# Fifteen pairs of projection tiles by seven block products instead of eight

## The chip, the cores and the metric

The kernel runs as one launch on one core of a Trainium2 chip. The metric is device time of one execution in microseconds (us). The inputs are in DRAM as fp32 and everything is computed to fp32 accuracy: an operand of a matrix product is split in a high and a low part that TensorE multiplies at its fast fp32 rate (type fp32r), and a product is the sum of high*high, high*low and low*high.

## What is computed

One layer of a hybrid encoder on 1024 prompt tokens and 64 tokens of a running stream, 1088 columns in all. One input projection feeds two branches:

```python
qa, ka, va, za, qkv_b, a_b, b_b, z_b, g_a, g_b = in_projection(x, w_in)   # x: 1088 x 1024
oa  = window_attention(rope(qa), rope(ka), va, sinks)      # 16 q heads, 4 kv heads of 64, chunks of 64 + 2 before
y_a = (oa * silu(za)) @ w_o_attn
qb, kb, vb = split(silu(causal_conv(qkv_b)))               # branch B: gated delta rule, 8 heads of 128
y_b = (rmsnorm(delta_rule(qb, kb, vb, decay(a_b), sigmoid(b_b))) * silu(z_b)) @ w_o_delta
h   = sigmoid(g_a) * y_a + sigmoid(g_b) * y_b
y   = layer_norm(ALPHA * x + h @ w_out)
```

The query `qa`, the branch-A gate `za` and the merge gates `g_a`, `g_b` are 1024 channels wide each: 8 + 8 + 16 tiles of 128 channels.

## The kernel before

The transposed input lies in SBUF for the whole run as eight tiles `ring` of [128, 2, 1088], one for each 128 input channels (a k-tile), high part and low part. Columns go in three groups, `GROUPS` = 384, 384 and 320. A **projection tile** gives 128 output channels for all columns: `weights` loads 128x1024 weights into `wraw`, splits them into `whi` (ScalarE copy, L85) and `wlo` (VectorE subtraction, L86), and `project`/`mm3` issue 3 groups x 8 k-tiles x 3 products = 72 matmuls. All matmuls go through `mm` (L103), transposes through L106, and TensorE takes them in the order of the program. PSUM has three buffers `pj` for projections and five `bg` for the rest. The other engines' order comes from priorities (`urgent` moves work ahead).

The stages, by the time in the profile:

- **Load and keys**, to 31.7 us. x arrives and is split, two key tiles are projected, and VectorE turns them by the rope table `cs` (`rope`), 1.1 MB that is read last of the load.
- **V and a/b** (`vab`), 31.7 to 58: 208 matmuls of 272 columns whose weights were split into a buffer of the pool `pla`, the pool of x's raw data.
- **Query**, 58 to 153: 8 tiles. Each column group is copied out of PSUM, turned (a shuffle and three VectorE operations), and split into high and low parts that go to DRAM (`q_d`). `gates`, the decays of branch B, run beside the first tile.
- **Branch-A gate**, 153 to 249: 8 tiles, silu into the SBUF tile `sz`. Beside it the keys are split, stored to `k_d` and read back into an SBUF tile `kp`.
- **Attention**, 249 to 503: 36 units (two heads of two kv heads, two chunks). `attention` issues the values of unit i-2, the flip (transposes of the probabilities P) of unit i-1, the scores of unit i, and then lets `weave` fill TensorE with `UNIT` = 8797 columns of 13 merge-gate tiles while P is made: VectorE takes maxima (`mx`, `nm`), ScalarE the exponentials (L479), VectorE the sums (`smm`) and the scaling (L485). A merge gate is copied to DRAM (`gA_d`, `gB_d`).
- **Branch B**, 503 to 1209: per pair of heads, the projections and the recurrence, filled with other projections. `GATES` = (0, 1, 1, 1) puts one of the last three merge-gate tiles behind each of pairs 1, 2 and 3.
- **Output**, 1209 to 1435.

## Time and profile before

| | before |
|---|---|
| time of three runs, us | median 1438.28 (1437.5 to 1438.64) |
| profiled execution, span from first to last instruction, us | 1434.8 |
| TensorE busy, us (share of span) | 1419.5 (99%) |
| VectorE busy | 896.1 (62%) |
| ScalarE busy | 536.0 (37%) |
| GpSimd busy | 152.2 (11%) |
| bytes moved by DMA | 147.47 MB |

The span is the profiled execution's own time as the profile gives it; the median of the timed runs is 3.5 us (0.2%) above it. In the views, PE is TensorE's matmuls, PEld its weight loads, DVE VectorE, ACT ScalarE, POOL GpSimd, SP the engine that issues most transfers. "L103" is a line of the kernel. PEclk is the clock that TensorE was granted, as a share of full speed.

### The profile page before, as it was taken

How to read it: one execution, taken by the hardware profiler on the slowest of the kernel's cores; microseconds unless marked ns; L12 is line 12 of the kernel's file. 1: busy time of each engine (PE TensorE's matmuls, PEld its weight loads, DVE VectorE, ACT ScalarE, POOL GpSimd, SP SyncE). 2: the span in 40 equal slices, each digit the busy share in tenths (PEclk: the TensorE clock that was granted, in tenths of full speed). 3: DMA queues.
4: the chain of work that ended last, by engine and by line, in shares of the span. 5: the costliest groups of instructions: out<-in, count | busy, mean ns of one | idle time of the engine just before them, and what ended most of it. 6: DMA issues, size and time to landing. Idle time of an engine off the chain costs nothing.

```text
span 1434.8 us, 28644 instructions
## 1 busy us (share of the span) xinstructions
PE 1419.5 (99%) x11362; PEld 1305.7 (91%) x11362; DVE 896.1 (62%) x2216; ACT 536.0 (37%) x1480; POOL 152.2 (11%) x321
## 2 busy tenths in 40 slices
PE   8999999999999999999999999999999999999997
PEld 8999999888888899988999889988999889999886
DVE  6477522555555447966696667866697444554676
ACT  5333311444444334345543555245534332322100
POOL 0000000000000014121231214021231100000000
PEclk9999999999999999999999999999999999999999
DMA  8134571333432321110222103211436326475221
GB/s 275 39 107 169 197 185 45 101 93 95 135 97 87 122 62 40 60 47 16 78 74 74 31 24 87 91 57 32 125 105 201 99 71 190 162 220 164 93 88 74
DMA packets 81172, 147.47 MB, mean 103 GB/s; under 512 B 10896, under 2 KB 60304, under 8 KB 79760
## 3 DMA queue, kind: packets, MB, share of 16 engines
q1 hardware_dynamic: 67552, 135.17, 29.6%
q10 hardware_dynamic: 13488, 10.49, 2.4%
q8 instruction: 89, 1.46, 0.4%
q14 instruction: 43, 0.35, 0.1%
HBM read 101.39 MB, written 44.24 MB: 102 GB/s over the span
## 4 chain that ended last, share of the span: by engine, by line
PE 98%; DVE 1%; ACT 1%; issue 0%; POOL 0%; DMA 0%; DVEq 0%; SPq 0%; ACTq 0%
PE pj L103 71%; PE bg L103 22%; PE bg L106 4%; PE pj L106 1%; DMA pl<-xT 0%; ACT whi L85 0%; DVE acc L582 0%; DVE whi L978 0%; ACT P L479 0%; POOL w1k L612 0%; ACT L319 0%; POOL ncv L575 0%; DVE whi L995 0%; DVE mx L468 0%; DVEq L1176 0%
## 5 line engine op out<-in xcount | busy, mean ns | idle before, releaser
L103 PE MATMUL pj<-ring,whi 128*128 128x384 f32 (+1 forms) x3696 | 929.8, 331 | 0.0
L103 PEld LDWEIGHTS pj<-ring,whi 128*128 128x128 f32 x3696 | 649.1, 188 | 3.1 <-issue 1.8
L103 PE MATMUL pj<-ring,wlo 128*128 128x384 f32 (+1 forms) x1848 | 610.6, 330 | 0.0
L103 PEld LDWEIGHTS pj<-ring,wlo 128*128 128x128 f32 x1848 | 347.7, 188 | 1.0 <-issue 0.7
L582 DVE SCALAR_TENSOR_TENSOR acc<-pre,sm,acc 128x384 f32<-128x384 f32 (+1 forms) x216 | 137.1, 640 | 24.9 <-ACT acc L580 21.5
L86 DVE TENSOR_TENSOR wlo<-wraw,whi 128x1024 fp32r<-128x1024 f32 (+2 forms) x86 | 101.0, 1175 | 80.4 <-ACT whi L85 74.2
L85 ACT ACTIVATE whi<-wraw 128x1024 fp32r<-128x1024 f32 (+2 forms) x86 | 87.6, 1018 | 114.5 <-PE pj L103 78.9
L103 PE MATMUL pj<-pl,ring 128*128 128x512 f32 (+2 forms) x432 | 94.5, 337 | 0.0
L103 PEld LDWEIGHTS pj<-pl,ring 128*128 128x128 f32 x432 | 68.4, 188 | 8.1
L479 ACT ACTIVATE P<-bg,nm 128x192 f32<-128x192 f32 (+2 forms) x136 | 54.4, 409 | 57.1 <-DVE nm L472 57.1
L785 DVE SCALAR_TENSOR_TENSOR S<-S,dec,bg 128x128 f32<-128x128 f32 x128 | 38.7, 344 | 54.5 <-PE bg L103 53.8
L103 PE MATMUL bg<-ring,whi 128*128 128x384 f32 (+1 forms) x240 | 61.3, 338 | 4.3 <-ACT ring L85 4.3
L583 ACT ACTIVATE gt<-acc 128x384 f32<-128x384 f32 (+1 forms) x72 | 36.5, 507 | 68.6 <-DVE acc L582 67.8
L588 DVE SCALAR_TENSOR_TENSOR plb<-gt,acc 128x384 f32<-128x384 f32 (+1 forms) x96 | 44.8, 483 | 22.8 <-ACT gt L583 22.7
L564 POOL MEMSET pre<- 128x3 f32 x24 | 2.4, 100 | 524.5 <-DMA prodA<-pl 476.6
L103 PEld LDWEIGHTS bg<-ring,whi 128*128 128x128 f32 x240 | 43.8, 192 | 6.2 <-ACT ring L85 4.8
L103 PE MATMUL bg<-PT,V 128*64 128x128 f32 (+1 forms) x496 | 48.1, 296 | 0.0
L580 ACT ACTIVATE acc<-pre,sm 128x384 f32<-128x384 f32 (+1 forms) x72 | 42.9, 597 | 12.9 <-DVE r17i L94 5.0
L103 PEld LDWEIGHTS bg<-PT,V 128*64 128x64 f32 (+1 forms) x496 | 24.3, 133 | 23.4 <-issue 21.2
L103 PE MATMUL pj<-wolo,ring 128*128 128x512 f32 (+1 forms) x120 | 45.0, 375 | 0.0
L795 ACT ACTIVATE w1k<-plb 128x128 f32<-128x128 f32 x68 | 21.0, 308 | 61.3 <-DVE plb L793 50.2
L480 DVE TENSOR_TENSOR smm<-smm,es 128x4 f32<-128x4 f32 (+1 forms) x36 | 5.8, 162 | 58.8 <-ACT P L479 58.8
(225 smaller groups left out, 1839.1 us busy)
## 6 DMA issues: line engine op xcount, KB each, us to landing
wraw<-w_tiles SPq DMA_DIRECT2D x80, 512.0 KB, 3.7
q_d<-pl SPq DMA_DIRECT2D x4, 2176.0 KB, 7.7
q<-q_d SPq DMA_DIRECT2D x64, 128.0 KB, 2.9
pl<-k_d SPq DMA_DIRECT2D x8, 512.0 KB, 8.0
prodA<-pl SPq DMA_DIRECT2D x2, 2048.0 KB, 7.9
t2k<-zs_d ACTq DMA_DIRECT2D x16, 256.0 KB, 2.8
prodB<-t2k ACTq DMA_DIRECT2D x16, 256.0 KB, 3.1
wraw<-w_out SPq DMA_DIRECT2D x8, 512.0 KB, 4.1
```

What stands on the lines that cost most here:

```text
L85: self.nc.scalar.activation(hi, raw, AF.Copy)
L86: self.nc.vector.tensor_tensor(lo, raw, hi.bitcast(F32), ALU.subtract)
L103: self.tc.keep_in_program_order(self.nc.tensor.matmul(o, l, r, start=start, stop=stop))
L106: self.tc.keep_in_program_order(self.nc.tensor.transpose(o, x, self.ident))
L479: nc.scalar.activation(P[:, hf, k], ps[:, k], AF.Exp, bias=nm[:, hf, b : b + 1], scale=0.125, accum_out=sm[:, hf, b : b + 1])
L480: nc.vector.tensor_tensor(sm[:, :, :nb], sm[:, :, :nb], es[:, :, :nb], ALU.add)
L580: nc.scalar.activation(acc[:, :w], pre[:, 0:w], AF.Copy, scale=cw(0))
L582: nc.vector.scalar_tensor_tensor(acc[:, :w], pre[:, j : j + w], cw(j), acc[:, :w], ALU.mult, ALU.add)
L583: nc.scalar.activation(th[:, :w], acc[:, :w], AF.Tanh, scale=0.5)
L588: nc.vector.scalar_tensor_tensor(o, v(th), 1.0, v(acc), ALU.add, ALU.mult)
L785: nc.vector.scalar_tensor_tensor(Sn[:, h], S[:, h], self.egl[h][:, p, c : c + 1], kv[:, 0:128], ALU.mult, ALU.add)
L795: nc.scalar.activation(junk, o, AF.Square, accum_out=d["sso"][:, c : c + 1])
```

## The change

Two neighbouring tiles (256 channels) are one product of a 2x2 block matrix of weights (blocks of 128 channels x 512 inputs, a11 to a22) with a 2x2 block matrix of x (512 inputs x 272 columns, B11 to B22, for each half g of the columns). It is now made by seven block products in place of eight. Eight sums of blocks feed it: T1 to T4 from x (made once, on GpSimd, `sums_x`) and s1 to s4 from each pair's weights (on GpSimd, `weights7`). One product is 12 matmuls of 272 columns (`product`), so a pair is 2 halves x 7 products x 12 = 168 matmuls of 272 columns; before it was 144 of 384 or 320. A PSUM buffer is read in the middle of a chain of products (`keep`, ScalarE), and the copies u are added to another product when it is done (`land`, VectorE). The 8 query, 8 branch-A gate and 14 merge-gate tiles go this way, 15 pairs; the rest stays.

T1 to T3 get a pool of their own (`rp2`). T4 is written over the odd quarters of the columns of four `ring` tiles at the end of `vab`, and `restore_x` reads x again after attention. To make room, the pool `pla` is closed after the keys and `vab`'s weights and the sums' operands come in a pool `vb` that begins where `pla` was; the pools `ws` (sums and splits of weights) and `rq` (query) begin where `vb` was, and the rope table is read a second time. Keys are split and stored as they are made (`put`, 44 stores of 64 partitions), through two buffers each of `khi` and `klo`; attention reads keys, query and branch-A gate from DRAM for each unit or pair of units. `GATES` becomes (0, 1, 1, 0): the last pair's merge-gate tile moves ahead into attention.

```diff
-GATES = (0, 1, 1, 1)
+GATES = (0, 1, 1, 0)
+    def sums_x(self):
...
+        for k in range(4):
+            xr = self.t(self.vb, [128, 2, NT], "xr", bufs=2)
+            nc.sync.dma_start(xr, self.I["xT"].rearrange("(h k) p n -> k p h n", h=2)[k])
...
+            for i, x, y in ((1, b12, b11), (2, b22, tm[1]), (3, b22, b12), (4, b21, tm[2])):
+                nc.gpsimd.tensor_tensor(tm[i], x, y, ALU.subtract)
+            for i in (2, 1, 3):
+                d = self.T[i, k] = self.t(self.rp2, [128, 2, 2, HN], "ring2", F32R, bufs=12)
+                self.split(d[:, 0], d[:, 1], tm[i])
+    def weights7(self):
...
+            sub(s1, a21, a22, ALU.add)
+            sub(s2, s1, a11, ALU.subtract)
+            sub(s3, a11, a21, ALU.subtract)
+            sub(s4, a12, s2, ALU.subtract)
+            for i, x in enumerate((a11, a12, s2, s1, s3, a22, s4)):
+                pool, tag, bufs = ((self.wp, "whi", 2), (self.wp, "wlo", 2), (self.ws, "wx", 3))[(0, 1, 2, 0, 1, 2, 2)[i]]
+                w = self.t(pool, [128, KT, 128], tag, F32R, bufs=bufs)
+                self.split(w[:, :4], w[:, 4:], x)
+    def product(self, ps, w, name, g, first, last):
+        hi, lo = w
+        for k in range(4):
+            xh, xl = self.operand(name, k, g)
+            for i, (l, r) in enumerate(((hi, xh), (hi, xl), (lo, xh))):
+                self.mm(ps[:, :HN], l[:, k], r, first and k == 0 and i == 0, last and k == 3 and i == 2, True)
+                yield HN
+    def stream(self, jobs):
...
+        for evac in jobs:
+            W = self.weights7()
+            for g in range(2):
+                cols = (2 * g * HN, (2 * g + 1) * HN)
+                A = self.pjt()
+                yield from self.product(A, W[0], "B11", g, True, False)
+                p1 = keep(A)
+                if tail:
+                    yield from tail
+                B = self.pjt()
+                yield from self.product(B, W[1], "B21", g, True, True)
+                evac(0, cols[0], B[:, :HN], p1)
+                yield from self.product(A, W[2], "T2", g, False, False)
+                u2 = keep(A)
+                C = self.pjt()
+                yield from self.product(C, W[3], "T1", g, True, False)
+                yield from self.product(A, W[4], "T3", g, False, False)
+                u3 = keep(A)
+                evac(1, cols[1], C[:, :HN], u3)
+
+                def rest(evac=evac, W=W, g=g, cols=cols, A=A, C=C, u2=u2):
+                    yield from self.product(A, W[5], "T4", g, False, True)
+                    evac(1, cols[0], A[:, :HN], None)
+                    yield from self.product(C, W[6], "B22", g, False, True)
+                    evac(0, cols[1], C[:, :HN], u2)
...
     def vab(self):
-        wt = self.t(self.pl, [128, 2, KT, 272], "pl", F32R)
+        wt = self.t(self.vb, [128, 2, KT, 272], "wt", F32R)
...
+        def put(gp, src, dst):
+            n = src.shape[-1]
+            for s, part in enumerate(self.key_parts(src)):
+                for hf in range(2):
+                    nc.sync.dma_start(self.k_d[gp, :, 2 * s + hf, dst : dst + n], part[HS[hf]].bitcast(F32))
...
+    def key_parts(self, src):
+        n = src.shape[-1]
+        parts = [self.t(self.pl, [128, 384], x, F32R, bufs=2)[:, :n] for x in ("khi", "klo")]
+        self.split(*parts, src)
+        return parts
...
         for hf in range(2):
-            ps = self.pjt() if hf else self.ps()
+            ps = self.ps()
```

**First place where instructions moved: ScalarE between the keys and `vab`.** `khi`/`klo` are the key parts on their way to DRAM, `wt` (before: `pl_45`) the split of `vab`'s weights, `V` the copy of its first result. A DMAHW name is the completion count of one of the eight lanes of SP's transfers. Before:

```order
L85 ACTIVATE ring_9_97<-pl_1_89 128x320
L85 ACTIVATE pl_45_413<-wraw_46_414 128x1088 [waits DMAHW6_49]
L273 DMA gt_48_422<-cg 128x256
L273 DMA gt_49_424<-cg 128x256 [waits Activation_49]
L85 ACTIVATE pl_45_413<-wraw_47_418 128x1088 [waits DMAHW7_49]
```

Now:

```order
L87 ACTIVATE khi_51_407<-rraw_47_392 128x64 [waits DMAHW5_49,DMAHW4_49]
L87 ACTIVATE khi_56_449<-rraw_54_442 128x256 [waits DMAHW0_49,DMAHW1_49,DVE_49,Activation_49]
L87 ACTIVATE khi_58_457<-rraw_54_442 128x64 [waits DMAHW5_49,DMAHW4_49,DVE_49]
L87 ACTIVATE khi_61_469<-ck_60_467 128x128 [waits DMAHW3_49,DMAHW2_49,DVE_49]
L87 ACTIVATE khi_63_477<-ck_60_467 128x128 [waits DMAHW7_49,DMAHW6_49,DVE_49]
L87 ACTIVATE wt_65_493<-wraw_66_494 128x1088 [waits DMAHW4_49,DMAHW3_49,DMAHW5_49,DMAHW2_49,DMAHW6_49,DMAHW1_49,DMAHW7_49,DMAHW0_49,DVE_49]
L87 ACTIVATE wt_65_493<-wraw_67_498 128x1088
L417 ACTIVATE V_68_502<-pj_103_590 128x256 [waits PE_49]
```

The split of `vab`'s weights stood behind the load of x and waited for its own data; it now stands behind the last key parts and waits for all eight lanes, on which the key stores are.

**Second place: ScalarE at the first pair of query tiles.** `sums` are s1 to s4, `whi`, `wlo`, `wx` the high parts of the pair's weights, `u` the copies of partial sums. Now (nothing of this stood there before):

```order
L417 ACTIVATE V_68_502<-pj_111_806 64x256
L418 ACTIVATE abt_69_503<-pj_111_806 64x16
L431 DMA cg0_113_844<-cg 128x128
L87 ACTIVATE whi_123_870<-sums_119_856 128x512
L87 ACTIVATE wlo_124_873<-sums_119_856 128x512
L87 ACTIVATE wx_122_867<-sums_119_856 128x512
L87 ACTIVATE wx_125_876<-wraw_118_854 128x512
L87 ACTIVATE wx_126_879<-sums_119_856 128x512
L349 ACTIVATE u_128_895<-pj_127_882 128x272
```

Three splits of sums stand between the end of `vab` and the first copy `u_128`, and the one that the next product takes (`wx_122`, s2) stands third.

**Third place: ScalarE within one unit of attention.** The L479 (now L644) rows are the four exponentials of one unit, `es` a small one of the sink, `PT` the copy of the flip. Before:

```order
L438 ACTIVATE gt_336_2781<-pj_324_2706 128x384
L479 ACTIVATE P_335_2769,smm_331_2750<-bg_332_2751,nm_329_2748 128x192
L474 ACTIVATE es_330_2749<-es_330_2749 128x4
L479 ACTIVATE P_335_2769,smm_331_2750<-bg_332_2751,nm_329_2748 128x192
L479 ACTIVATE P_335_2769,smm_331_2750<-bg_333_2752,nm_329_2748 128x192 x2
L85 ACTIVATE whi_386_3065<-wraw_385_3064 128x1024
L438 ACTIVATE gt_338_2809<-pj_337_2784 128x320
```

Now, in another unit:

```order
L644 ACTIVATE P_646_4198,smm_642_4179<-bg_643_4180,nm_640_4177 128x192
L639 ACTIVATE es_641_4178<-es_641_4178 128x4
L644 ACTIVATE P_646_4198,smm_642_4179<-bg_643_4180,nm_640_4177 128x192
L349 ACTIVATE u_647_4220<-pj_596_3943 128x272
L87 ACTIVATE wlo_657_4248<-sums_652_4231 128x512
L644 ACTIVATE P_646_4198,smm_642_4179<-bg_644_4181,nm_640_4177 128x192
L349 ACTIVATE u_661_4270<-pj_660_4257 128x272
L644 ACTIVATE P_646_4198,smm_642_4179<-bg_644_4181,nm_640_4177 128x192
L571 ACTIVATE gs_649_4224<-gs_648_4222 128x272
L668 COPY PT_662_4292<-bg_663_4293 128x3x128
```

The fill's splits and copies stood behind the four exponentials; now two copies and a split stand between them.

## Rows read from the trace of the kernel before

**Rows 1.** Page, parts 1, 4 and 5: busy time, chain by engine, weight loads.
```profile
PE 1419.5 (99%) x11362; PEld 1305.7 (91%) x11362; DVE 896.1 (62%) x2216; ACT 536.0 (37%) x1480; POOL 152.2 (11%) x321
...
PE 98%; DVE 1%; ACT 1%; issue 0%; POOL 0%; DMA 0%; DVEq 0%; SPq 0%; ACTq 0%
...
L103 PEld LDWEIGHTS pj<-ring,whi 128*128 128x128 f32 x3696 | 649.1, 188 | 3.1 <-issue 1.8
```

**Rows 2.** Busy time by stage; columns: stretch, length, engines with instruction counts, clock, DMA.
```profile
31.70:58.00 26.30, 26.30 (x211) 26.30 (x210) 11.09 (x29) 6.25 (x21) 0.00 (x0) 1.00 0.12 37
58.00:153.00 95.00, 94.89 (x578) 94.57 (x577) 70.15 (x156) 33.04 (x63) 0.00 (x0) 1.00 0.32 116
153.00:249.00 96.00, 96.00 (x586) 96.00 (x585) 27.68 (x42) 22.22 (x36) 0.00 (x0) 1.00 0.54 154
249.00:503.00 254.00, 253.15 (x1882) 222.30 (x1880) 139.25 (x451) 107.16 (x403) 0.00 (x0) 1.00 0.33 104
```

**Rows 3.** Chain of waits, from 1200 to 1240: start, length, what.
```profile
1209.07 14.92 PE pj L103 x93
1223.99 12.00 PE bg L103 x72
```

**Rows 4.** Timeline of VectorE behind the keys: start, length, operation, idle before.
```profile
30.96 0.56 DVE L351 TENSOR_TENSOR rsh<-rsh,cs 128x384 f32<-128x384 f32 x1 [5.40 <-DMA cs<-rope]
31.44 0.55 DVE L352 TENSOR_TENSOR rraw<-rraw,cs 128x384 f32<-128x384 f32 x1
...
32.72 1.23 DVE L86 TENSOR_TENSOR wlo<-wraw,whi 128x1024 fp32r<-128x1024 f32 x1 [0.27 <-ACT whi L85]
...
42.52 0.56 DVE L376 TENSOR_TENSOR kT<-rraw,rsh 128x256 f32<-128x256 f32 x2
```

**Rows 5.** Transfers from 20 to 60: issues, KB each, median us to landing.
```profile
cs<-rope SPq DMA_DIRECT2D x1, 1088.0 KB, 6.6
...
o_nkp<-kT SPq DMA_DIRECT2D x1, 128.0 KB, 2.2
```

**Rows 6.** Timeline of SP: the length is that of one issue.
```profile
33.98 0.33 SPq L141 DMA_DIRECT2D wraw<-w_tiles  x1
```

**Rows 7.** VectorE and ScalarE by shape, query stage: busy, mean ns, idle before.
```profile
L86 DVE TENSOR_TENSOR wlo<-wraw,whi 128x1024 fp32r<-128x1024 f32 x8 | 9.8, 1225 | 5.6 <-ACT whi L85 5.6
L350 DVE STREAM_SHUFFLE rsh<-rraw 128x384 f32<-128x384 f32 x16 | 9.5, 591 | 0.0
...
L85 ACT ACTIVATE whi<-wraw 128x1024 fp32r<-128x1024 f32 x8 | 8.5, 1057 | 1.6 <-issue 1.6
L85 ACT ACTIVATE pl<-rraw 128x384 fp32r<-128x384 f32 x15 | 7.9, 525 | 32.5 <-DVE rraw L407 32.5
L349 ACT ACTIVATE rraw<-pj 128x384 f32<-128x384 f32 x16 | 7.7, 482 | 6.2 <-PE pj L103 6.2
```

**Rows 8.** GpSimd by shape, whole span: two-input operations of 512 columns.
```profile
L705 POOL TENSOR_TENSOR U<-V,sm 128x512 f32<-128x512 f32 x16 | 16.9, 1059 | 64.1 <-DVE V L734 63.9
```

**Rows 9.** Timeline of one unit of attention.
```profile
345.23 1.12 PE L103 MATMUL bg<-pl,q 128*128 128x192 f32 x8
345.24 0.48 ACT L503 COPY PT<-bg 128x384 f32<-128x384 f32 x1 [1.66 <-PE bg L106]
...
349.75 1.01 DVE L485 TENSOR_SCALAR P<-P,smm 128x192 f32<-128x192 f32 x4
...
351.85 0.55 PE L106 MATMUL bg<-cf,P 128*128 128x128 f32 x3
```

**Rows 10.** One VectorE line with two inputs in SBUF: shortest, median, longest ns.
```profile
L582 DVE SCALAR_TENSOR_TENSOR acc<-pre,sm,acc x216: 541/618/1358, 515.2 to 1062.8; 128x384 f32<-128x384 f32 x73, 128x323 f32<-128x323 f32 x35
```

**Rows 11.** Timeline of GpSimd and VectorE at one long instance of that line.
```profile
568.22 1.06 POOL L705 TENSOR_TENSOR PB<-P,sm 128x512 f32<-128x512 f32 x1
568.34 1.35 DVE L582 SCALAR_TENSOR_TENSOR acc<-pre,sm,acc 128x384 f32<-128x384 f32 x1
```

**Rows 12.** Busy time at the end of the run, columns as in Rows 2.
```profile
1428.00:1431.00 3.00, 0.00 (x0) 0.00 (x0) 2.93 (x12) 0.00 (x0) 0.00 (x0) 0.78 0.00 0
```

More of the change, by code (lines that the diff above doesn't have):

```diff
@@ L36 @@
 PBW = 6 * NT
[L37 removed]
+EARLY, LATE, LATER = (0, 1, 2, 3, 4, 5, 6, 7), (2, 3, 4, 5, 6, 7, 0, 1), (4, 5, 6, 7, 0, 1, 2, 3)
 KW = SEQ + 128 + DEC
+HN = NT // 4
+QUARTERS = tuple((i * HN, HN) for i in range(4))
 SWAPMASK = [i + 8 if i < 8 else i - 8 if i < 16 else i for i in range(32)]
@@ new lines, in product, with keep @@
+    def product(self, ps, w, name, g, first, last):
+        hi, lo = w
+        for k in range(4):
+            xh, xl = self.operand(name, k, g)
[3 more added lines that the diff above has]
+    def stream(self, jobs):
+        nc = self.nc
+        tail = None
+        def keep(ps):
+            u = self.t(self.ws, [128, HN], "u", bufs=4)
+            with self.urgent():
+                nc.scalar.activation(u, ps[:, :HN], AF.Copy)
+            return u
+        for evac in jobs:
[22 more added lines that the diff above has]
+                    evac(0, cols[1], C[:, :HN], u2)
+                tail = rest()
+        yield from tail
@@ L261, in vab, with land @@
+    def land(self, dst, ps, add):
+        with self.urgent():
+            if add is None:
+                self.nc.scalar.activation(dst, ps, AF.Copy)
+            else:
+                self.nc.vector.tensor_tensor(dst, ps, add, ALU.add)
     def vab(self):
         nc, I = self.nc, self.I
-        wt = self.t(self.pl, [128, 2, KT, 272], "pl", F32R)
+        wt = self.t(self.vb, [128, 2, KT, 272], "wt", F32R)
         hi, lo = wt[:, 0], wt[:, 1]
```

267 lines of the change are left out of this document (167 added, 100 removed).

## Prediction

> **What bounds the kernel now.** I read the page's busy times and chain first: TensorE is busy 99% of the span and is 98% of the chain that ended last [rows 1]. So time saved on TensorE counts in full only as long as nothing new makes it wait, and every new wait of TensorE counts in full too. Then the stages: in query, gate and attention TensorE is busy throughout, but VectorE is busy 70 of 95 us in the query stage, 28 of 96 in the gate stage and 139 of 254 in attention [rows 2]. The reader is to see that the query stage has the least VectorE room. Last I read the places where the new order makes TensorE depend on others: the end of the keys, the first pair, a unit of attention.
>
> **The gain.** A tile now takes 12.0 us by the chain [rows 3]; 8 tiles in 96 us with 586 matmuls recorded give 11.8 [rows 2]; I take 11.8, so 23.6 a pair. For 272 columns the V stage is the row: 211 matmuls in 26.3 us, 0.125; I take 0.126, so 168 x 0.126 = 21.15 a pair. That saves 2.45 us x 15 pairs = **-36.8 us** (bounds -34 and -40 by 11.7 and 12.0 a tile).
>
> **Keys to V: +22 us (16 to 25).** Before, V's matmuls followed the keys at once, and VectorE turned the keys beside them: the rope table came at 30.96, and the last key operation began at 42.52 and ended at 43.1, with one 1.23 us split of weights in between, so 10.9 us of rope [rows 4]. Now the split `wt` waits until all key stores have landed, and TensorE's next matmul is V's; what is queued behind `wt` on ScalarE is V's own copies. The table still comes at about 31. The six rope groups, with four splits of key parts between them (0.55 each and waits for ScalarE), end at about 43.8. Behind that stand the splits and stores of the last pieces through two buffers each. A round through both buffers is four issues by SP at 0.33 [rows 6], a landing of 2.2 [rows 5] and splits of 0.2 to 0.4, so about 3.2; three rounds end at 53.4. The split of 1088 columns takes 1.1 (1057 ns for 1024 [rows 7]), so TensorE, idle since 31.7, starts at about 54: 22 to 23 us, I take 22. If the stores of different rounds overlapped fully, the last four issues and one landing behind 43.8 would give 47.3 and TensorE 16 us of idle; if the landing takes 3 us, 25. The sums T of x, 16 GpSimd operations of 544 columns at about 1.1 (from 1059 ns for 512 [rows 8]), start only then too, but with 26 us of V beside them they end about when V does: nothing, and up to 3 if each waits for its load.
>
> **V to the first pair: +6 (3 to 9).** The sums of weights need V's buffers, so they start at V's end: four at 1.06 [rows 8]. TensorE has 24 matmuls, 3.0 us, that need no sum. ScalarE splits s1, then s3 (ready at 3.3), then s2, a22, s4, at 0.63 each (by 1057 and 525 ns for 1024 and 384 [rows 7]), and only then copies u_128, at about 6.2, on which the T2 product waits: 3.2 idle. The decays of branch B follow with their table loads on ScalarE while the second read of the rope table (6.6 to land [rows 5]) holds VectorE's rope; I add 3.
>
> **Query: +9 (3 to 14).** VectorE operations start 0.48 apart at 384 columns [rows 4]; by 1225 ns for 1024 [rows 7] a column costs about 1 ns, so 0.36 at 272 and 0.61 at 512. A pair has eight pieces of 272 with a shuffle (591 ns at 384 [rows 7], so about 0.4), four two-input operations and about 0.1 for the dependence: 8 x 1.94 = 15.5. Six landings of 0.4 and seven splits of 0.61 come on top: 22.2. GpSimd's four sums a pair cost VectorE something: one line with two SBUF inputs takes 618 ns as a rule but 1358 at most [rows 10], and a long instance (1.35) lies beside a GpSimd sum of 1.06 that began just before [rows 11]. I take 0.3 a sum, nearer to the median than to the longest, and get 23.4 a pair, against 21.15 on TensorE: 4 x 2.25 = 9. Below: 0.75 a pair if VectorE's backlog drains into the gate stage. Above: the whole 0.73 that the long instance lost, four times a pair, 25.1.
> The Trainium skill (SBUF — State Buffer, Who interferes with whom) says that a VectorE instruction with two SBUF inputs and a GpSimd instruction that reads SBUF exclude each other and the second blocks for the whole first. The long instance agrees (0.12 us behind the start of a 1.06 us sum it lost 0.73); the median shows that it is rare. By the rule each sum could cost its full 1.06 and a query pair would be 26.4.
>
> **Gate stage: 0.** VectorE and ScalarE are at 28 and 22 of 96 us [rows 2]; landings, splits and copies add about 10 us of each to a pair of 21.
>
> **Attention: +8 (3 to 22).** In the unit shown the scaling of P ends at 350.76 and the flip starts at 351.85, and the two last scalings (0.5) are needed only by its second half: about 1.35 us of slack [rows 9], and 0.17 more as the fill is 33 matmuls of 0.126 and not 4.0 us. What the order puts into this chain: of 36 units 20 have between their exponentials a copy (0.37) or split (0.63) on ScalarE, at most 1.6 us, and 20 have a landing or split on VectorE between the exponentials' sum and the last scaling. Added up by unit, seven pass the slack, by 0.1 to 0.9: 3 us. New is also that the second score product of every second unit takes the PSUM buffer that the flip's ScalarE copy of the same unit has just read: a copy of 0.48 starts about when the scores start, and two score matmuls (0.25) cover it [rows 9], so 0.3 x 18 = 5. Below, 3; above, each fill product whose PSUM copy queues behind exponentials may cost TensorE about 0.5 (28 times), 22 in all.
>
> **The rest: +2 (0 to 5).** Idle of 20 us lowers the clock: with no matmul, 1428 to 1431 shows a granted clock of 0.78 [rows 12], on the way from 2.4 to 1.2 GHz, so V's first matmuls are slower; 1 us. Reading x again behind attention: its first use is behind 1.5 us of another product and half the k-tiles, hidden; 1 us. GATES: with the 12.0 us tile gone, 14.9 us of matmuls still stand at the end [rows 3] as cover for the last norm; without cover the price would be up to 12.
>
> Sum: -36.8 + 22 + 6 + 9 + 8 + 2 = +10.2, a span of 1445.0 from 1434.8. The median of the runs lay 3.5 above the span: **1448.5 us**.
>
> **The rivals.**
> *The vector engines keep up.* Backlog in the query stage drains into the gate stage and attention's added work falls into gaps. For it: the low VectorE share of the gate stage [rows 2]. Against: two buffers for a rope piece hold only some 4 us of backlog. The two terms together would be 3 rather than 17: span 1431, 1434.5. From 3.9 downward the change is faster by over 0.2%, so this one ends on the other side.
> *The key stores drain early*, as at the lower bound of 16: 1442. At 8.9 us of idle the kernel would be measurably faster; that needs stores without buffer rounds, against the order's rows of waits.
> *GpSimd's sums block VectorE and the chain of attention*: each sum takes the 0.73 of the long instance [rows 11], so a query pair is 25.1, +16, and the 28 sums in attention fall on units without slack, +20 on top of 8: 1475.5. That is what the rule of the Trainium skill's page SBUF — State Buffer would lead to; for it speaks the long instance, against it the median of 618 ns [rows 10].
> *Nothing waits*: 1434.8 - 36.8 + 3.5 = 1401.5. Against it: `wt`'s wait on all lanes.
> *The products are no cheaper.* If weight loads set the pace (one for each matmul, 188 ns [rows 1]), 168 x 0.188 would be 31.6 a pair, 1434.8 + 15 x 8 + 3.5 = 1558 before any wait; the V stage at 0.125 [rows 2] speaks against.
>
> **How the numbers follow.** Chances: the sum as worked out 0.60, vector engines keep up 0.18, early stores 0.06, GpSimd blocks 0.12, nothing waits 0.03, no cheaper 0.01. A measurement here can tell 0.2% (2.9 us) from no change. Faster: most of the second, the fifth and a low end of the first, 0.24; same 0.10; slower 0.66. The range goes down to the lower bounds of query and attention and a key wait of 18 (1448.5 - 6 - 5 - 4 = 1433.5), and of the first pair and the rest (5 less, 1428); it goes up to the upper bounds of query and attention together (1467.5) and a key wait of 24.5 (1470). The likeliest case alone spans 1438 to 1462.
>
> **What would show it.** Idle of TensorE of 20 us or more between keys and V, released by ScalarE `wt` behind transfers; idle of some 3 us at the first T2 product released by ScalarE's u; query pairs at 23 to 24 us with VectorE near full; 0.3 us waits on PT's copy in attention; gate pairs at 21.2. Wrong would be it if the key stores land by 45, or if a gate pair is not 21.2 us.

## The result and the profile after

| | before | after |
|---|---|---|
| median of the runs, us | 1438.43 (1437.5 to 1438.64) | 1501.16 (1499.97 to 1503.35) |
| span of the profiled execution, us | 1434.8 | 1500.1 |

The change is slower: ratio 1.0443, 95% interval 1.0428 to 1.0458. The forecast had the direction right; its time, 1448.5, and its range, up to 1470, are far too low. The products themselves became cheaper as forecast; the loss is idle time, short waits and a lower clock of TensorE.

The page after, parts 1 and 4, busy time and chain by engine; the lines answer to [rows 1]:

```profile
PE 1414.9 (94%) x11722; PEld 1292.3 (86%) x11722; DVE 1011.7 (67%) x2463; ACT 605.8 (40%) x1687; POOL 256.2 (17%) x397
...
PE 64%; DVE 3%; ACT 2%; DMA 2%; issue 1%; SPq 0%; POOL 0%; DVEq 0%; ACTq 0%
```

The chain after the change is followed back over 72% of the span only, to some 420 us, so its shares don't stand against those of before, where TensorE was 98% of the whole span. VectorE has 116 us more work, GpSimd 104. TensorE's busy time fell by 4.6 us and not by the 36.8 that the products save: a matmul at a lower clock is busy for longer (further down, 17 of them in 3.67 us). The next view is what TensorE waited for after the change (in all, times, longest):

```profile
PE pj L105 <- ACT wt L87: 29.4, 1, 29.4
PE bg L108 <- DVE P L650: 7.4, 11, 1.2
PE pj L105 <- ACT u L349: 6.2, 4, 4.1
PE pj L105 <- DVE rraw L387: 5.7, 5, 2.4
PE pj L105 <- ACT gs L571: 4.6, 5, 1.9
PE pj L105 <- POOL tm L274: 4.6, 1, 4.6
```

The busy time by stage after the change, columns as in [rows 2]: the idle time before V, the start of V, the rest of V, query, gate, attention, and what follows.

```profile
31.70:61.20 29.50, 0.10 (x1) 0.02 (x1) 10.88 (x30) 6.03 (x14) 0.88 (x3) 0.57 0.41 92
61.20:70.00 8.80, 8.24 (x46) 7.93 (x47) 2.49 (x2) 1.51 (x4) 4.10 (x4) 0.69 0.95 343
70.00:98.00 28.00, 22.33 (x166) 21.91 (x165) 14.94 (x18) 12.73 (x32) 19.03 (x13) 0.94 0.27 89
98.00:206.00 108.00, 96.34 (x711) 93.64 (x710) 104.79 (x253) 46.86 (x107) 27.75 (x20) 0.95 0.54 132
206.00:287.50 81.50, 79.28 (x624) 78.41 (x623) 46.82 (x88) 34.98 (x78) 21.15 (x16) 1.00 0.46 130
287.50:575.30 287.80, 272.54 (x2184) 238.04 (x2182) 184.67 (x532) 138.79 (x502) 30.46 (x24) 0.96 0.51 140
575.30:1500.00 924.70, 908.84 (x7860) 827.66 (x7858) 627.29 (x1500) 347.82 (x915) 149.04 (x308) 0.99 0.29 92
```

From these and [rows 2] the ledger follows. The length that a stage should have had is that of before less the tiles that left it at 11.8 us and plus the pairs that came at 21.15: query and gate 191.0 - 8 x 2.45 = 171.4, attention 254.0 - 13 x 11.8 + 7 x 21.15 = 248.7, the rest 931.8 - 11.8 = 920.0.

| stage | without any new wait | measured | lost | forecast to be lost |
|---|---|---|---|---|
| keys to the end of V | 26.3 | 66.3 | +40.0 | 23 (22 idle, 1 clock) |
| first pair, query and gate | 171.4 | 189.5 | +18.1 | 15 (6 and 9) |
| attention | 248.7 | 287.8 | +39.1 | 8 |
| the rest | 920.0 | 924.8 | +4.8 | 1 |
| sum | | | +102.0 | 47 |
| gain of 15 pairs | | | -36.8 | -36.8 |

102.0 - 36.8 = 65.2 of the 65.3 us between the two spans. That the two agree is no proof of the gain, since "lost" is counted from the lengths with the gain already taken off. Two stages hold nearly all of the error: keys to V (17 us more than forecast) and attention (31 more).

**Keys to V.** The timeline of SP after the change, first and last of the 22 rows of key stores (start, length, operation):

```profile
30.47 1.11 SPq L500 DMA_DIRECT2D k_d<-khi  x2
...
57.22 1.18 SPq L500 DMA_DIRECT2D k_d<-klo  x2
59.97 0.40 SPq L269 DMA_DIRECT2D xr<-xT  x1
```

The stores stand back to back from 30.5 to 58.4: 44 stores in 27.9 us with four small outputs among them, 0.6 us for one. The forecast priced an issue at 0.33, from a load of a whole tile of weights [rows 6]. SP hardly waited for a landing or a buffer (its longest gap is 0.5 us, at 48.0); it was busy issuing. Behind the stores the split follows at once (timeline of ScalarE), and GpSimd's sums of x, whose reads stand behind the stores on SP, start at 65.8 (timeline of GpSimd, the first and the last rows of them):

```profile
60.00 2.11 ACT L87 ACTIVATE wt<-wraw 128x1088 fp32r<-128x1088 f32 x2 [7.13 <-DMA k_d<-klo]
```
```profile
65.82 2.69 POOL L274 TENSOR_TENSOR tm<-xr 128x544 f32<-128x544 f32 x2 [33.24 <-DMA wraw<-w_tiles]
...
90.96 2.76 POOL L274 TENSOR_TENSOR tm<-xr,tm 128x544 f32<-128x544 f32 x2
```

A sum takes 1.35 to 1.83 here, not 1.1, and the last ends at 93.7. V, which took 26.3 us before, takes 36.8. Of the 10.5 more, 6.2 are waits: 4.6 on `tm`, 1.0 on a PSUM copy behind the splits of T (`abt`), 0.5 on the second half of `wt`. The rest is the clock: 0.50 (1.2 GHz) in the first 4 us of V, behind the long idle stretch, and 0.58 from 94 to 98, behind the wait on `tm`; the shares below 1.00 add up to 2.7 and 1.7 us.

**Query.** VectorE is busy 104.8 of 108.0 us. From 125 to 206, three stretches of 27 us, TensorE's 562 matmuls make 24.2 us a pair (168), near the forecast's 23.4. VectorE by shape, first in the query stretch, then in the gate stretch, where the last two of the same operations fall (busy, mean ns):

```profile
L481 DVE TENSOR_TENSOR rsh<-rsh,cs 128x272 f32<-128x272 f32 x30 | 16.4, 548 | 0.5
```
```profile
L481 DVE TENSOR_TENSOR rsh<-rsh,cs 128x272 f32<-128x272 f32 x2 | 0.9, 436 | 0.0
```

**Attention.** One unit after the change on three engines: the first and the last of GpSimd's four sums of a pair's weights, then VectorE, then TensorE (three timelines).

```profile
338.94 1.29 POOL L321 TENSOR_TENSOR sums<-wraw 128x512 f32<-128x512 f32 x1 [36.04 <-DVE wx L88]
...
342.77 1.39 POOL L321 TENSOR_TENSOR sums<-wraw,sums 128x512 f32<-128x512 f32 x1
```
```profile
339.47 0.78 DVE L645 TENSOR_TENSOR smm<-smm,es 128x4 f32<-128x4 f32 x1 [0.26 <-ACT P L644]
...
340.50 3.78 DVE L650 TENSOR_SCALAR P<-P,smm 128x192 f32<-128x192 f32 x4
```
```profile
341.72 0.30 PE L108 MATMUL bg<-cf,P 128*128 128x128 f32 x1 [0.25 <-DVE P L650]
342.86 0.77 PE L108 MATMUL bg<-cf,P 128*128 128x128 f32 x3 [0.84 <-DVE P L650]
344.33 0.69 PE L108 MATMUL bg<-cf,P 128*128 128x128 f32 x2 [0.70 <-DVE P L650]
```

The four scalings of P took 1.01 us before [rows 9]; beside the sums they take 3.78, about one in each sum, and the flip comes out of TensorE in three pieces with 1.8 us of idle between them. What follows is seen in a fine table of the same stretch (columns as in [rows 2]; the clock is the third number from the end):

```profile
336.00:340.00 4.00, 4.00 (x34) 3.85 (x35) 3.04 (x8) 2.89 (x12) 1.06 (x1) 1.00 0.56 193
340.00:344.00 4.00, 2.53 (x20) 1.23 (x20) 3.93 (x6) 0.91 (x3) 3.92 (x4) 0.89 0.20 72
344.00:348.00 4.00, 3.67 (x17) 3.67 (x18) 2.85 (x8) 0.40 (x2) 0.16 (x1) 0.50 0.22 66
```

After the idle pieces the granted clock is 0.50, 1.2 GHz, and in 4 us TensorE does 17 matmuls where it did 34 in the first row. The clock falls so at four of the six places in attention where GpSimd has sums, at 300, 340, 470 and 512; at the other two, 387 and 425, it does not. In tables of 4 us the share of clock below 1.00 adds up to 3.4, 3.4, 1.7 and 1.7 us at the four, 10.2 in all, which bounds what the clock cost from above, since it also counts time in which TensorE stood idle. It comes on top of 7.4 us of waits on P (0.8 before). How much the clock matters shows in the kernel with eight buffers for key parts (below), whose attention is the same program with the same waits on P, 7.6 us:

```profile
290.90:570.80 279.90, 265.56 (x2184) 230.91 (x2182) 182.76 (x532) 138.53 (x502) 30.60 (x24) 0.99 0.52 144
```

There the clock falls at one place only, for 1.7 us by the same count, and attention is 7.9 us shorter than 287.8. At 470 the way is another one: two small operations ahead of the exponentials, `nm` (1.26 us) and `es` (1.22), are stretched, the exponentials are late, and behind them on ScalarE the copy `u`, for which TensorE waits 1.26.

The same in one line each, shortest, median and longest ns of the scaling of P and of `es`, an operation on 4 columns, after the change (the scaling's longest was 324 before):

```profile
L650 DVE TENSOR_SCALAR P<-P,smm x136: 242/315/1330, 292.4 to 567.2; 128x192 f32<-128x192 f32 x120, 128x64 f32<-128x64 f32 x8, 128x128 f32<-128x128 f32 x8
```
```profile
L638 DVE TENSOR_TENSOR es<-nm,nsink x36: 155/161/1218, 290.5 to 565.2; 128x4 f32<-128x4 f32 x32, 128x2 f32<-128x2 f32 x4
```

The medians are those of before, 315 and 161, and the longest is about a whole GpSimd sum. The Trainium skill (SBUF — State Buffer, Who interferes with whom) says that whichever of VectorE and GpSimd gets the shared port first holds it for a whole instruction while the other blocks, and that this concerns not only VectorE operations with two inputs but also `tensor_scalar` in its two-port modes. The 1330 ns of the scaling agree; the prediction had used the rule for two inputs alone.

### The profile page after: what moved, and what is told of

It reads as the page before. It is cut to its first block, busy times and chain, and to the rows that moved or that the text cites. A ratio compares the mean times of both kernels' runs of the same rounds, so it can differ in the third digit from the quotient of the medians.

```text
span 1500.1 us, 30407 instructions
## 1 busy us (share of the span) xinstructions
PE 1414.9 (94%) x11722; PEld 1292.3 (86%) x11722; DVE 1011.7 (67%) x2463; ACT 605.8 (40%) x1687; POOL 256.2 (17%) x397
## 4 chain that ended last, share of the span: by engine, by line
PE 64%; DVE 3%; ACT 2%; DMA 2%; issue 1%; SPq 0%; POOL 0%; DVEq 0%; ACTq 0%
PE pj L105 44%; PE bg L105 17%; PE bg L108 3%; DMA wraw<-w_tiles 2%; ACT P L644 1%; DVE ring L88 1%; ACT whi L87 0%; DVE mx L635 0%; DVE wlo L88 0%; DVE acc L747 0%; DVE es L638 0%; DVE P L650 0%; SPq L1072 0%; DVE t2k L835 0%; ACT PT L668 0%
## 5 line engine op out<-in xcount | busy, mean ns | idle before, releaser
L105 PE MATMUL pj<-ring,whi 128*128 128x384 f32 (+2 forms) x2928 | 673.7, 325 | 5.0 <-DVE gt L1059 2.4
L105 PEld LDWEIGHTS pj<-ring,whi 128*128 128x128 f32 x2928 | 486.7, 190 | 8.7 <-issue 4.2
L105 PE MATMUL pj<-ring,wlo 128*128 128x272 f32 (+2 forms) x1824 | 474.6, 318 | 9.8 <-ACT gs L571 4.6
L105 PEld LDWEIGHTS pj<-ring,wlo 128*128 128x128 f32 x1824 | 306.1, 191 | 14.2 <-ACT gs L571 5.9
L105 PE MATMUL pj<-ring,wx 128*128 128x272 f32 x1080 | 152.6, 293 | 8.6 <-ACT u L349 4.6
L105 PEld LDWEIGHTS pj<-ring,wx 128*128 128x128 f32 x1080 | 143.0, 192 | 10.1 <-ACT u L349 5.3
L87 ACT ACTIVATE whi<-wraw 128x1024 fp32r<-128x1024 f32 (+2 forms) x71 | 65.2, 918 | 75.8 <-PE pj L105 45.8
L88 DVE TENSOR_TENSOR wlo<-wraw,whi 128x1024 fp32r<-128x1024 f32 (+2 forms) x56 | 64.3, 1149 | 39.9 <-ACT whi L87 33.9
L644 ACT ACTIVATE P<-bg,nm 128x192 f32<-128x192 f32 (+2 forms) x136 | 54.5, 409 | 43.0 <-DVE nm L637 37.7
L105 PE MATMUL pj<-pl,ring 128*128 128x512 f32 (+1 forms) x240 | 70.1, 375 | 0.0
L105 PE MATMUL pj<-wt,ring 128*128 128x272 f32 x192 | 27.1, 305 | 31.0 <-ACT wt L87 29.4
L349 ACT ACTIVATE u<-pj 128x272 f32<-128x272 f32 x90 | 35.5, 395 | 45.9 <-PE pj L105 45.2
L105 PEld LDWEIGHTS pj<-wt,ring 128*128 128x128 f32 x192 | 26.3, 203 | 31.8 <-issue 29.6
L105 PE MATMUL bg<-ring,wlo 128*128 128x384 f32 (+1 forms) x144 | 49.2, 341 | 0.2 <-DVE wlo L88 0.2
```

What stands on the lines that cost most here:

```text
L87: self.nc.scalar.activation(hi, raw, AF.Copy)
L88: self.nc.vector.tensor_tensor(lo, raw, hi.bitcast(F32), ALU.subtract)
L105: self.tc.keep_in_program_order(self.nc.tensor.matmul(o, l, r, start=start, stop=stop, skip_group_check=skip))
L349: nc.scalar.activation(u, ps[:, :HN], AF.Copy)
L644: nc.scalar.activation(P[:, hf, k], ps[:, k], AF.Exp, bias=nm[:, hf, b : b + 1], scale=0.125, accum_out=sm[:, hf, b : b + 1])
```

## The experiments

Each kernel is the changed one with the edit shown. The kernel before took 1436.7 to 1436.9 us on the same chips. All but the last are single executions; the runs of the changed kernel spread over 3.4 us, so totals are read to some 3 us and stages from the traces. Attention is less steady than the other stages: in the six kernels below that change nothing in it (three on key stores, two on V's space, one on query) it takes 279.9 to 288.3 us, so a difference there says little under some 8 us.

### Keys to V

**V's weights in a place of their own.** The key tiles move from the pool `pla` into a pool `kb` behind a pad, so that what V writes no longer waits for key stores.

```diff
-                with scope("pla") as self.pl:
+                with scope("pla") as self.pl, scope("pad") as pad, scope("kb") as self.kb:
+                    self.t(pad, [128, PAD], "pad")
...
-        parts = [self.t(self.pl, [128, 384], x, F32R, bufs=2)[:, :n] for x in ("khi", "klo")]
+        parts = [self.t(self.kb, [128, 384], x, F32R, bufs=2)[:, :n] for x in ("khi", "klo")]
```

> Key parts lie where no later tile of V's stage comes (a pad tile between the pools), so V's weights no longer wait for the key stores; nothing else is changed. Theory: the 29.4 us wait goes from the start of V (61.2 to about 32), but three of the four reads of x for the sums T still stand behind the 44 stores on SP, which issue at 0.64 us each until about 58, so the wait comes back at the first T2 product and the whole gains little, 3 to 12 us (1489 to 1498). Rival: the wait was the whole loss there, and the whole gains 29 us or more (1472 or less).

1497.5 us. By stage (V, then up to the first T2 product), and the longest wait of TensorE:

```profile
31.70:58.07 26.37, 26.37 (x209) 26.15 (x208) 17.72 (x33) 10.13 (x32) 6.50 (x6) 1.00 0.44 100
58.07:99.30 41.23, 3.51 (x25) 3.10 (x25) 20.57 (x25) 11.24 (x24) 23.14 (x16) 0.59 0.39 127
```
```profile
PE pj L106 <- ACT wx L88: 37.6, 1, 37.6
```

V runs as before the change, at full clock, and the wait of 29.4 is gone. The time is not: TensorE then waits 37.6 us at the first T2 product for GpSimd's sums of x, whose reads are still behind the stores on SP. So the wait of `wt` was one of two waits behind the same stores, and removing it alone gives 3.7 us, as expected.

**The same, and the reads of x issued by GpSimd.**

```diff
-            nc.sync.dma_start(xr, self.I["xT"].rearrange("(h k) p n -> k p h n", h=2)[k])
+            nc.gpsimd.dma_start(xr, self.I["xT"].rearrange("(h k) p n -> k p h n", h=2)[k])
```

> As the first, and the four reads of x for the sums T are issued by GpSimd and not by SP. Theory (two things in a row on SP's issues, the stores and then the reads): V runs 32 to 58, T is ready when V ends, the first T2 product starts near 62, the whole is 36 to 42 us shorter than the change (1459 to 1465). Rival (GpSimd's sums themselves are the bound, 16 at 1.4 us and splits between them): T is ready only at 70 or later and the gain is under 30 (1471 or more).

1485.5 us, 15.7 less than the changed kernel. The T2 product starts at 85.07 instead of 105.2 (99.3 in the run above), after 11.3 us of idle for `abt`. The larger gain was missed: T2 starts late enough for the rival, GpSimd's sums as the bound. The keys end 7.7 us later than in the run above, with the reads of x beside the load; and the table shows the stretch from the end of V to T2:

```profile
65.80:85.07 19.27, 5.20 (x25) 4.99 (x25) 17.11 (x20) 9.54 (x23) 13.42 (x9) 0.64 0.30 90
```

GpSimd is busy 13.4 and VectorE 17.1 of 19.3 us: sums, then their splits. The sums of x do not fit beside V as the forecast had it.

**The low parts stored from ScalarE's queue.**

```diff
-                    nc.sync.dma_start(self.k_d[gp, :, 2 * s + hf, dst : dst + n], part[HS[hf]].bitcast(F32))
+                    (nc.sync, nc.scalar)[s].dma_start(self.k_d[gp, :, 2 * s + hf, dst : dst + n], part[HS[hf]].bitcast(F32))
```

> Half of the key stores (those of the low parts) are issued by ScalarE and not by SP; V's weights still wait for all of them. Theory (44 issues on one queue at 0.64 us are the length of the wait): the last store lands near 46 to 48 and V starts near 49 to 51 in place of 61.2; the whole is 8 to 12 us shorter than the change (1489 to 1493). Rival (the two buffers for key parts and the 2 us of landing set the length, as the prediction had it): V starts at 55 to 58, the whole 1495 or more.

1498.9 us; V starts at 59.7 after 27.9 of waiting, not ten earlier, so neither the theory nor the rival's 55 to 58 came out. The timeline of ScalarE shows why halving SP's issues gave so little:

```profile
32.70 2.46 ACTq L500 DMA_DIRECT2D k_d<-klo  x4
35.26 0.87 ACT L508 ACTIVATE rraw<-bg 128x384 f32<-128x384 f32 x2 [2.51 <-DMA k_d<-klo]
```

An issue costs ScalarE 0.6 us too, in its own stream, and the copies that VectorE's rope needs stand behind four of them.

**Eight buffers for the key parts, one queue; and eight buffers with both queues.**

```diff
-        parts = [self.t(self.pl, [128, 384], x, F32R, bufs=2)[:, :n] for x in ("khi", "klo")]
+        parts = [self.t(self.pl, [128, 384], x, F32R, bufs=8)[:, :n] for x in ("khi", "klo")]
```

> Eight buffers for the key parts in place of two, all stores still on SP. Theory (either limit alone is about 28 us: 44 issues at 0.64, or the rounds through two buffers): V still starts at 58 to 61, the whole within 4 us of the change (1497 or more). Rival (the buffers are the limit): V starts at 52 or earlier, the whole 1492 or less.

> Eight buffers for the key parts, and the stores of the low parts issued by ScalarE. Theory (two limits of equal length, both taken away): V starts at 46 to 51, the whole 9 to 15 us shorter than the change (1486 to 1492). Rival (a third limit, VectorE's rope and splits or ScalarE's issues in its own stream): V at 54 or later, the whole 1494 or more.

With one queue 1495.0 us: ScalarE's last key split ends at 43.1, but the stores still end at 59.0 and V starts at 61.8. So the rounds through two buffers, on which the forecast built, are not the bound, and the stores stand on SP back to back as before. (The total is 6 us under the changed kernel's, less than expected; that lies in attention, 279.9 us here, and not in the keys or V.) With both queues 1499.8: V starts at 57.7, later than the theory and on the rival's side, and ScalarE's stream is again where the time stands, at the end of the keys, where the next split waits 4.91 us for eight issues:

```profile
46.40 5.09 ACTq L500 DMA_DIRECT2D k_d<-klo  x8
```

No kernel with fewer or cheaper issues was run; that V would start earlier with them is argued from the timelines.

### Query

**The four query pairs without GpSimd's sums.** Plain blocks stand in for s1 to s4, so the products are those of other weights; everything else runs.

```diff
-            sub = lambda d, x, y, op: nc.gpsimd.tensor_tensor(d, x, y, op)
+            if self.wn <= 10:
+                s1, s2, s3, s4 = a21, a11, a21, a12
+            sub = lambda d, x, y, op: nc.gpsimd.tensor_tensor(d, x, y, op) if self.wn > 10 else None
```

> In the four query pairs alone the GpSimd sums are left out (plain blocks in their place). Theory (sums lengthen VectorE's two-input operations, mean 548 ns at 272 columns in the query stage against 436 in the gate stage): the query stage loses 8 to 13 us and the wait for the first T2 product 3 more; the whole 1487 to 1491. Rival (VectorE is the bound by its own work): the stage changes by less than 4 us, the whole 1494 or more.

1489.4 us, as expected; query and gate take 178.1 in place of 189.5. Both stages, and the line of VectorE that took 548 ns in the query stage:

```profile
99.56:277.68 178.12, 171.15 (x1333) 168.52 (x1331) 138.71 (x338) 81.36 (x184) 26.60 (x20) 1.00 0.52 139
```
```profile
L483 DVE TENSOR_TENSOR rsh<-rsh,cs 128x272 f32<-128x272 f32 x31 | 14.2, 458 | 0.7 <-DMA cs<-rope 0.2
```

Of the 11.4 us, 3.7 lie before the first T2 product, which here starts 3.6 us behind V's end instead of 7.2 and waits for no sum. The 7.7 behind it are 0.48 for each of 16 sums, more than the 0.3 that the forecast took and less than the whole 0.73 of the long instance [rows 11]. VectorE's own times agree: the four two-input operations of a piece are 258 ns shorter together, 7.7 us over 30 pieces.

### Attention

**The 14 merge-gate tiles in the old way**, x read again before attention; and **the same with the flip's second half in `pj` again.**

```diff
-            for i in range(0, 16 - sum(GATES), 2):
-                yield gate((self.gA, self.gB)[i // 8], i % 8, False)
...
-                            self.weave(self.attention(), work)
-                            self.drain(work)
-                        self.restore_x()
+                        self.drain(work)
+                        self.restore_x()
+                        self.order = LATER
+                        gates = self.gate_project(range(16 - sum(GATES)))
+                        with scope("at") as self.at:
+                            self.mp = self.at
+                            self.weave(self.attention(), gates)
+                            self.drain(gates)
```
```diff
-            ps = self.ps()
+            ps = self.pjt() if hf else self.ps()
```

> The 14 merge-gate tiles are made the old way (72 matmuls a tile, splits of 1024 columns) in attention, with x put back before attention; keys, query and gate are still streamed and the flip still takes two bg buffers. Theory (the seven-product fill's splits, copies and landings stand in attention's chain): attention, 287.8 us for 14 tiles, falls to 266 to 272, although its matmuls cost 16.8 us more than seven pairs; the whole 1480 to 1488. Rival (streaming from DRAM and the PSUM buffers slow attention): attention stays at 285 or more and grows by the matmuls, the whole at 1500 to 1515.

> The run with the old merge-gate tiles, with the flip's second half in a pj buffer again, as before the change; keys, query and gate are still streamed. That run needed 266 us of attention for 13 tiles (the 14th came behind it) where the kernel before needed 254. Theory (with both halves of the flip in bg, the second score product waits for the copy of the flip of its own unit): attention falls by 7 to 12 us, the whole to 1483 to 1488. Rival (streaming keys, query and gate is the cost): attention falls by less than 4, the whole 1491 or more.

1495.1 and 1488.2 us. Attention with 13 old tiles, first with the flip in `bg`, then in `pj`:

```profile
292.15:558.00 265.85, 260.33 (x1883) 226.20 (x1881) 142.49 (x457) 108.58 (x406) 0.00 (x0) 0.99 0.55 154
```
```profile
291.60:551.50 259.90, 256.24 (x1883) 225.05 (x1881) 142.38 (x457) 108.65 (x406) 0.00 (x0) 0.99 0.57 157
```

The flip's buffer is worth 6.0 us (forecast 5; the theory of this run had 7 to 12, its rival under 4). The second is 5.9 above the 254.0 of before; 3.4 of it is a wait at the start for the first gate tile's weights, whose load stands behind the reading of x, and behind that wait the clock is low, over the next 4 us:

```profile
295.60:299.60 4.00, 3.35 (x9) 2.85 (x10) 2.08 (x2) 2.78 (x11) 0.00 (x0) 0.50 0.89 291
```

With 0.66 in the 4 us after it that is up to 3.4 us more, so little or nothing is left that keys, query and gate from DRAM would have cost. The whole of the first kernel came out higher than expected because the fourteenth tile runs behind attention with nothing beside it.

**The first merge-gate pair's weights for all pairs**: no loads, sums or splits of weights in attention. The other six pairs multiply by the first pair's weights, and every later tile reads weights 12 places before its own in the list; the amount of work behind attention is the same.

```diff
-        for evac in jobs:
-            W = self.weights7()
+        for j, evac in enumerate(jobs):
+            if j <= 8:
+                W = self.weights7()
```

> The weights of the first merge-gate pair are used for all seven pairs, so six pairs' weight loads, sums on GpSimd and 42 splits are left out of attention; products, copies u, landings and tanh stay. Theory (splits and sums are the larger part of what delays the chain): attention 287.8 to 268 or less, the whole 1481 or less. Rival (the copies, landings and PSUM buffers are the larger part): attention 278 or more, the whole 1491 or more.

1477.3 us. Attention takes 264.2, 23.6 less (15.7 less than the shortest of the kernels that change nothing in it), at a clock of 1.00 throughout, and the listed waits of TensorE are 2.2 us in all of it, 0.4 of them on P:

```profile
288.60:552.80 264.20, 260.62 (x2184) 229.14 (x2182) 145.26 (x490) 117.20 (x460) 0.00 (x0) 1.00 0.47 128
```

**The two halves of this apart**: first loads and splits without sums, then loads and sums without splits (in both, the merge gates are products of other weights).

```diff
+            if self.wn > 16 + 2:
+                s1, s2, s3, s4 = a21, a11, a21, a12
+            sub = lambda d, x, y, op: nc.gpsimd.tensor_tensor(d, x, y, op) if self.wn <= 18 else None
```
```diff
+            W = self.weights7(None if j <= 8 else W)
...
+            if old:
+                return old
```

> In the seven merge-gate pairs the four GpSimd sums of a pair are left out and plain weight blocks stand in their place; all loads, 49 splits and products stay. Theory (the sums hold VectorE's second SBUF read and so lengthen attention's chain): attention falls from 287.8 to 272 or less, the whole to 1485 or less. Rival (the splits in the queues of ScalarE and VectorE are the cause): attention 280 or more, the whole 1493 or more.

> The counterpart: in attention the weights of all pairs are loaded and the four sums made on GpSimd, but from the second merge-gate pair on no split is made of them, the first pair's weights are used. Theory (sums are the cause): attention stays at 280 or more, the whole at 1493 or more. Rival (splits are the cause): attention near the 264.2 of the run with the weights made once, the whole 1480 or less.

1484.8 and 1497.9 us. Attention without sums, then with sums alone, and in the latter one wait of TensorE that no other kernel has (timeline of TensorE):

```profile
288.80:561.00 272.20, 263.73 (x2184) 230.31 (x2182) 169.67 (x532) 138.38 (x502) 0.00 (x0) 0.99 0.54 148
```
```profile
288.25:571.30 283.05, 266.03 (x2184) 233.44 (x2182) 156.56 (x490) 117.62 (x460) 30.11 (x24) 0.97 0.51 142
```
```profile
337.19 3.08 PE L105 MATMUL pj<-ring,whi 128*128 128x272 f32 x12 [10.02 <-DVE gs L389]
```

Loads and splits alone cost 272.2 - 264.2 = 8.0, and leaving the sums out takes attention 7.7 us below the shortest of the kernels that change nothing in it, close to the theory's 272. What sums alone cost the second kernel doesn't settle. It is 18.9 more than without either, but 10.0 of it is the one wait, which belongs to this kernel's own order on SP: the addition `gs` waits 7.4 us for the store of a gate, issued at 332.9 behind loads of weights. And the clock behind that wait, 0.50 and 0.64 over 8 us, costs up to 3.4 more. That leaves 5.5 to 8.9. Together weights cost 23.6; that this is more than the sum of the two parts is not clear of what attention changes by itself.

### The branch-A gate alone

**Only the branch-A gate by seven products.** Query and merge gates go the old way, with V's weights in a place of their own, the flip in `pj`, the sums of x made beside the query and x read again before attention.

```diff
...
+                    with scope("rq") as self.rq:
+                        self.load_rope(self.rq)
+                        self.query(self.gates(abt))
                     with scope("ws") as self.ws:
...
+                        self.drain(self.front())
...
```

> Seven products only where vector engines and order have room: the branch-A gate, 4 pairs. Query and merge gates the old way, flip's second half in pj, key parts where no later tile comes, the sums T on GpSimd beside the query stage, x put back before attention. Theory: 4 x 2.45 = 9.8 us less on TensorE in the gate stage, the sums T cost VectorE in the query stage some 12 us that lie in its 25 us of room, 3.5 us of wait for x, a few for streaming: 1430 to 1440, equal to the kernel before or some us faster. Rival (streaming, the second read of the rope table or the start of the gate stage cost more than 10): 1445 or more.

1474.89 us (1474.06 to 1475.95), ratio to the kernel before 1.0264, interval 1.0247 to 1.0281, far on the rival's side. By stage (query, gate), the beginning of the gate stage in TensorE's timeline (its first matmuls and its first T2 product), and TensorE's longest waits in the query stage:

```profile
58.10:177.75 119.65, 101.82 (x588) 100.89 (x586) 93.81 (x173) 41.93 (x81) 26.32 (x16) 0.93 0.60 153
177.75:278.10 100.35, 88.57 (x676) 87.16 (x674) 50.09 (x92) 40.03 (x87) 21.62 (x16) 0.93 0.38 107
```
```profile
177.75 1.67 PE L106 MATMUL pj<-ring,whi 128*128 128x272 f32 x12
190.55 0.82 PE L106 MATMUL pj<-ring,wx 128*128 128x272 f32 x2 [9.64 <-ACT wx L88]
```
```profile
PE pj L106 <- ACT rraw L430: 10.1, 2, 6.9
PE bg L106 <- DMA cg<-cg: 7.8, 1, 7.8
```

The gate stage takes 100.4 us, 4.4 more than the 96.0 of before. It has 9.6 of wait for the first split of a sum of weights, and in the 4 us from 192 on a clock of 0.50. Without that wait it is 90.7, 5.3 less than before; four pairs should have given 9.8. The query stage takes 119.7 and not 95.0 [rows 2]: 10.1 us of waits on the copies of the query while GpSimd makes the sums of x beside them, 7.8 for a transfer of `gates`, and a clock of 0.93. What has to be made for the products cost more than they gave in either place that was tried for it, and no version tried here beats the kernel before.

## Why the prediction was wrong

**The gain held.** -36.8 us by 21.15 a pair. It is seen where nothing else limits, in the gate stage after the change:

```profile
228.00:250.00 22.00, 21.72 (x173) 21.50 (x172) 11.57 (x22) 9.54 (x22) 5.14 (x4) 1.00 0.45 127
```

The next 22 us have 172 matmuls with 21.72 us busy, so 168 take 21.1 to 21.2, and 21.4 to 21.5 with the idle. Weight loads do not set the pace.

**Keys to V: the wait was foreseen, its price was not.** The step that failed is "a round through both buffers is four issues by SP at 0.33". A 64-partition key store takes SP 0.6, 44 of them 27.9 us, and the kernel with eight buffers shows that the buffers had no part in it. The price stood in the trace of before: the issue of `o_nkp`, the row whose landing the prediction took, is 0.61 there, and 72 loads of `q` have a median of 0.60. (The round was added up wrongly too: four issues, a landing and splits of 0.2 to 0.4 are 3.7 to 3.9, not 3.2, which would have put V at 56.) Issues end to end from 30.5 on, 44 at 0.6 and the small outputs, with the prediction's own landing and split behind the last, would have given about 30. The second part of the error is V itself, 10.5 us longer where the forecast had 1 for the clock. The step is the sentence on the sums of x: "nothing, and up to 3". They cost 4.6 of wait on `tm`, 1.0 on `abt` and the low clock behind, up to 1.7; the clock behind the long idle stretch, put at 1, was up to 2.7. The sentence gave the sums 1.1 us and V's whole time as cover, and did not ask what stands ahead of their reads on SP. The kernel with V's weights apart shows that the sums end the wait on their own: TensorE then stands 37.6 us at T2.

**The first pair and query: 18.1 for 15.** The first stall at T2 was 4.1 (forecast 3.2), released by ScalarE's `u` as expected. The mechanism was right; the term that was too small is "I take 0.3 a sum": the runs gave 0.48, 2.9 us more over 16 sums, and with it a pair is 24.1 by the prediction's own sum, as measured (24.2). Even without sums TensorE was not fully covered: 171.2 busy of 178.1.

**Attention: 39.1 for 8, the largest error.** Its two named parts were the flip's PSUM buffer, 5, measured 6.0, and the chain of P, 3. The second failed: it added up what the order put between the exponentials on ScalarE and VectorE, unit by unit, at undisturbed durations. It left out that GpSimd's sums stretch the scaling of P, an operation with one tensor input that [rows 10] said nothing about, from 1.01 to 3.78 for four, and that TensorE's clock falls behind a flip in pieces, up to 10.2 us. Weights made beside attention cost 23.6, that clock included, since without them it is 1.00 throughout. How the 23.6 divide between sums and splits is known only roughly (8.0 for loads and splits alone, 5.5 to 8.9 for sums alone). Of what is left, 39.1 - 23.6 = 15.5, the flip's buffer is 6.0, if it is worth the same beside pairs as beside old tiles. The other 9.5 go with the pairs' products, since the kernel with old tiles in attention doesn't have them; whether it is the copies `u`, their additions or the PSUM buffers that a pair holds stays open. All these are differences from one trace of 287.8; the same attention took 279.9 in another kernel, mostly by the clock.

**The rest: 4.8 for 1.** At the start of branch B TensorE waits 3.2 us for the split `whi`, which itself waits for its weights to land, and later 2.4 for `gt`, where it waited for neither before. The prediction called the second reading of x "hidden"; it is what delays these weights, by the buffer that both use. The reading fills both `wraw` buffers, and its splits (timeline of ScalarE) stand behind the last product that reads T4:

```profile
572.22 2.30 ACT L87 ACTIVATE ring<-wraw 128x544 fp32r<-128x544 f32 x4 [0.73 <-PE pj L105]
```

Branch B's first weights are issued on SP only at 574.30, where before the change they were issued 5 us ahead of that stage. Behind the wait the granted clock is 0.50 and 0.57 over 7 us.

**The rivals.** The one on GpSimd blocking VectorE, at 12 in 100, had the right mechanism. Its price was too high in query (0.73 a sum, measured 0.48) and about right in attention: 20 us for the sums, where leaving them out gave 287.8 - 272.2 = 15.6, the clock included, which it did not think of. At 1475.5 it missed mostly because it kept the forecast's price for keys to V. Little of "vector engines keep up" was seen, although VectorE is at 57% in the gate stage: the last two rope pieces fall into that stage, but TensorE waits 7.1 us in query for reads of its PSUM buffers by VectorE and ScalarE (`rraw`), so a backlog cannot wait that long.

## What to carry to other kernels

Price a transfer's issue by its own shape and count what each queue must issue in a row: 44 small stores are 28 us of one queue, whatever the bytes, and everything issued behind them is late too. An engine that was idle (GpSimd here) is not free help where VectorE's chain has a microsecond of slack; look for the longest instance of an operation beside the idle engine's work, and price each collision by that. A buffer that a new transfer borrows is not there for the transfer that used it before, even far from the place that was changed. Saving TensorE's work at the cost of gaps can cost twice, because behind most of the longer gaps here it ran for a few us at 1.2 GHz instead of 2.4.

## What was not expected of the hardware

- An issue of a 64-partition store to DRAM takes 0.6 us on SP and on ScalarE alike, against 0.33 to 0.40 for a load of a whole tile; on ScalarE its next copy waits for it.
- GpSimd's sums of weights, 512 columns, take 1.26 to 1.39 us, against 1059 ns for another operation of 512 columns in [rows 8]. VectorE is not the reason: in the kernel with sums alone one took 1.26 at 334.8, while VectorE stood idle. VectorE's four-column `es` goes from 161 to 1218 ns in the worst instance.
- After three idle pieces of TensorE, 1.8 us together, the granted clock was 0.50 over the next 4 us, in which TensorE was busy throughout but for 0.3. With the same waits on P (7.4 and 7.6 us) the clock fell at four places of attention in one kernel and at one in another.
